# Attention keys with a meta key in front of every row, and right neighbours moved one element to the left by DMA

## The chip, the cores and the metric

The kernel runs on one NeuronCore of a Trainium2 chip. The metric is the device time of one execution in microseconds. The kernel is written with a framework that records instructions, finds their dependencies and writes the semaphores. The engines are TensorE (PE, with its weight loads PEld), VectorE (DVE), ScalarE (ACT), GpSimd (POOL) and SyncE (SP), which here only issues transfers. Each engine takes its instructions in a fixed order.

## The reference, cut to what matters

One layer of a bidirectional encoder: an input projection, then two branches side by side (a neighbourhood attention and a gated linear recurrence), a gated merge, an output projection and an MLP, over 1024 real tokens and 16 learned meta tokens. The change touches the attention alone. The tokens form a grid of 16 rows by 64 columns; a query attends to a clamped window of 8 rows by 16 columns around it, with a relative bias, and always to all 16 meta keys:

```python
col_start = jnp.clip(c - NA_WIN_W // 2, 0, GRID_W - NA_WIN_W)
in_win = (c[None, :] >= col_start[:, None]) & (c[None, :] < col_start[:, None] + NA_WIN_W)
s_win = jnp.where(in_win[:, None, :], s_win + bias[None], -1e30)
s_meta = jnp.einsum('brchd,bmhd->bhrcm', qg, km).astype(jnp.float32) * scale
s = jnp.concatenate([s_win.reshape(B, H, rows, GRID_W, kh * GRID_W), s_meta], axis=-1)
p = jax.nn.softmax(s, axis=-1).astype(v.dtype)
o_grid = (jnp.einsum('bhrcjw,brjwhd->brchd', p_win, v_blk)
          + jnp.einsum('bhrcm,bmhd->brchd', p_meta, vm)).reshape(B, T, H, dh)
```

There are 8 heads of 64. A query in column c sees columns c−8 to c+7, shifted inwards at the grid's edges.

## The kernel before, in words

All matrix products are in a rounded fp32 format with each operand split into a high and a low part; the product of the two low parts is left out.

**Stages.** The recurrence comes first (until about 340 us), then the attention with the projections of its queries, keys and values (until about 571 us), then the gates, the merge, the output projection and the MLP. Four head pairs are done one after the other in the attention (the loop over `p`, L766). A pair's projections (`proj`, L133) put out queries, keys and values in that order; the next pair's projections are there to fill PE while the present pair's softmax runs.

**Strips.** The 64 columns are cut into 8 strips of 8 columns. A strip holds 16 rows × 8 columns = 128 tokens, one full tile of partitions. A query strip `s` needs the key strips `s−1`, `s` and `s+1`; the edge strips 0 and 7 have two. `KS` and `KL` (high and low keys) hold for each strip 128 real keys and then 16 meta keys (`SW` = 144 columns), so that three strips are one run of 432 columns, of which only the centre strip's meta columns are unmasked. `QX` holds the query's high part on one half of the partitions and its low part on the other.

**Scores** (L831): two products into one bank (L838, L839), 432 columns wide (288 at the edges). DVE adds mask and bias from `NB` and takes the minimum (L844), ACT takes the exponent (L846), DVE scales (L847, L848).

**Values** (L851): the probabilities `pr` are turned block by block by transposes on PE (L859), with one more transpose that is shifted by 16 columns and so ends with the meta columns (L861). ACT copies the high part to `PH` and DVE the low part to `PL` (L870, L871). After every four strips (a group: 2 halves of strips × 2 heads in a pair) the products with the values follow: first and last with the ninth block of `V`, which holds the meta values in its last 16 rows and zeros elsewhere (L875, L884), in between with each block of `V` that the four strips see (L882, L883). `V` has nine blocks of 128 tokens (2 heads × (64 high + 64 low) columns); it is one buffer, filled for each pair by transposes of `vT` (L821) and copies by ACT and DVE (L823, L824).

**Order.** In this stage the order on the engines is not written out by hand (a written order for PE, ACT and DVE ends with the first pair's keys, `in_order.close()`). A planner puts an instruction on its engine when its inputs and buffers are ready by the planner's own reckoning, earlier code first; the order is fixed when the kernel is built. Transfers for weights (L102, L951), bias (`bs`, L770) and mask (`NB`, L771) are on SP's queue. A value step runs when three score steps stand ahead of it (`pend`, L892 to L896); there are five tiles of probabilities, two banks for scores, and one `PT` a head for high and one for low parts.

Of the kernel before, what the change touches and what calls it, by code (L numbers as in the profile page):

```python
# [9 lines left out]
F32 = mybir.dt.float32  # L10
F32R = mybir.dt.float32r
# [25 lines left out]
SW = P + NM  # L37

# [10 lines left out]
def layer(ctx: ExitStack, tc: tile.TileContext, x, meta, w_in, w_na, w_hg, w_o, w_up, w_dn,  # L49
# [697 lines left out]
    with (tc.tile_pool(name="npr", bufs=1, side="right", reuse_waits="tile") as npr,  # L747
# [5 lines left out]
        V = npr.tile([P, 9, 2, P], F32R, name="Vn")  # L753
        pool.memset(KL[0][64:128].bitcast(F32), 0.0)
        pool.memset(KL[1][0:64].bitcast(F32), 0.0)
        pool.memset(vT[:, 8], 0.0)

        def strips(t, p0, t0, n, w=None):

            a = t[p0:p0 + 64, 0:8, t0 // 8:(t0 + n) // 8]  # L760
            return a.rearrange("p s (r c) -> p s r c", c=8)

# [3 lines left out]
        for p in range(NPAIR):  # L766
            NB = npl.tile([P, 2, 1024], F32, tag="NB", name="NB")
            for i in range(2):
                bs = npl.tile([P, TH], F32, tag="bs", name="bs", bufs=3)[:, :384]
                sp.dma_start(bs, bias[:, (2 * p + i) * 384:(2 * p + i + 1) * 384])  # L770
                sp.dma_start(NB[:, i, :1008], wmask)  # L771
                for o, j0, m in ((0, 0, 3), (432, 1, 2), (720, 0, 2)):
                    a = NB[:, i, o:o + m * SW].rearrange("p (j c) -> p j c", c=SW)[:, :, :P]
                    pool.tensor_tensor(a, a, bs[:, j0 * P:(j0 + m) * P].rearrange("p (j c) -> p j c", c=P),
                                       op=ALU.subtract)
# [14 lines left out]
            def ev_k(ps, t0, n):  # L790
                for i in range(2):
                    act.copy(strips(KS[i], 64 * i, t0, n), grid(ps, 64 * i))
                for i in range(2):
                    b = 64 * i
                    dve.tensor_tensor(strips(KL[i], b, t0, n), grid(ps, b),
                                      strips(KS[i], b, t0, n).bitcast(F32), op=ALU.subtract)
                    act.copy(strips(KS[i], 64 - b, t0, n), strips(KS[i], b, t0, n).bitcast(F32))

            def mev_k(ps):
                for i in range(2):  # L800
                    b = 64 * i
                    m = ps[b:b + 64].unsqueeze(1).broadcast_to([64, 8, NM])
                    hi = KS[i][b:b + 64, :, P:]
                    act.copy(hi, m)
                    act.copy(KS[i][64 - b:128 - b, :, P:], m)
                    dve.tensor_tensor(KL[i][b:b + 64, :, P:], m, hi.bitcast(F32), op=ALU.subtract)
# [10 lines left out]
            for b in (0, 4, 8):  # L817
                pt = bank("t", "vpt")
                m = min(4, 9 - b)
# [4 lines left out]
                dve.tensor_tensor(V[:, b:b + m, :, 64:], src, V[:, b:b + m, :, :64].bitcast(F32), op=ALU.subtract)  # L824

# [5 lines left out]
            def scores(s, i):  # L831
                js = [j for j in (s - 1, s, s + 1) if 0 <= j < 8]
                w = len(js) * SW
                o = 432 if s == 0 else 720 if s == 7 else 0
                sc = bank("s", "nsc").rearrange("p a b -> p (a b)")
                ksl = KS[i][:, js[0]:js[-1] + 1].rearrange("p s c -> p (s c)")
                kll = KL[i][:, js[0]:js[-1] + 1].rearrange("p s c -> p (s c)")
                pe.matmul(sc[:, :w], QX[i][:, s], ksl, start=True, stop=False)  # L838
                pe.matmul(sc[:, :w], QX[i][:, s], kll, start=False, stop=True)  # L839
                pr = npr.tile([P, 432], F32, tag="pr", name="pr", bufs=5)  # L840
# [8 lines left out]
                return js, pr  # L849

            def values(s, i, js, pr):  # L851
                g, e = divmod(s, 4)
                if e == 0:
                    po[i] = [npr.tile([P, 22, P], F32R, tag=f"PT{q}", name=f"PT{q}") for q in range(2)]
                PH, PL = po[i]
                m = len(js)
                pt = bank("t", "ppt")
                for k in range(m):
                    pe.transpose(pt[:, k], pr[:, k * SW:k * SW + P], ident)  # L859
                cen = js.index(s)  # L860
                pe.transpose(pt[:, m], pr[:, cen * SW + NM:cen * SW + NM + P], ident)  # L861

                b0 = 3 * (js[0] - 4 * g) + e + 3
                if s < 7:
                    runs = [(0, m + 1, b0)]
                else:
                    runs = [(0, m, b0), (m, 1, 4 * e + 9)]
                for k, n, b in runs:
                    hi = PH[:, b:b + 3 * n - 2:3]
                    act.copy(hi, pt[:, k:k + n])  # L870
                    dve.tensor_tensor(PL[:, b:b + 3 * n - 2:3], pt[:, k:k + n], hi.bitcast(F32), op=ALU.subtract)  # L871
# [3 lines left out]
                pe.matmul(ov, V[:, 8, i], PH[:, 9:22:4], start=True, stop=False)  # L875
                for a in range(-1, 5):
                    j = 4 * g + a
                    if 0 <= j < 8:
                        es = [q for q in range(4) if abs(a - q) <= 1]
                        e0, ne = es[0], len(es)  # L880
                        b = 3 * a + e0 + 3
                        pe.matmul(ov[:, e0:e0 + ne], V[:, j, i], PH[:, b:b + ne], start=False, stop=False)  # L882
# [997 lines left out]
```

## Time and profile before

| what | value |
|---|---|
| time, median of 3 runs | 1510.95 us (1508.72 to 1511.25) |
| the profiled execution | 1510.21 us |
| its span, first to last instruction | 1508.4 us |
| PE busy | 1493.8 us, 99% of the span |
| DVE, ACT, POOL busy | 69%, 44%, 24% |
| mean granted TensorE clock | 0.999 |
| attention stage (340 to 571 us): PE, DVE, ACT busy | 228.87, 175.62, 144.91 of 231 us |

Busy time is the time in which an engine has at least one instruction under way. Matrix products overlap in their pipeline: what one of them holds PE for is the time from its start to the next one's start, not its listed duration. "Idle before, releaser" names what ended a wait. For transfers the page gives the number, the size and the median time from issue to landing.

### The profile page before, as it was taken

The page shows a single profiled execution, that of the slowest core. Times are in us where ns is not written, and L with a number is a line of the kernel's source. Part 1 is how long each engine was busy: PE and PEld are TensorE (multiplying, and loading weights), DVE is VectorE, ACT ScalarE, POOL GpSimd, SP SyncE. Part 2 cuts the span into 40 slices and gives each one's busy share as a digit, 9 for nine tenths or more (in the row PEclk, how much of TensorE's full clock was granted, in tenths as well). Part 3 has the DMA queues.
Part 4 walks back from the last instruction along what each step waited for, and adds up shares of the span by engine and source line. Part 5 has one row for each costly group of instructions (what it writes and reads, how often), then busy time and mean ns, then how long its engine had stood idle before and what let it go on. Part 6 is the DMA issues. An engine that isn't in the chain of part 4 may idle for free.

```text
span 1508.4 us, 23495 instructions
## 1 busy us (share of the span) xinstructions
PE 1493.8 (99%) x9200; PEld 1251.0 (83%) x9200; DVE 1036.5 (69%) x1624; ACT 664.7 (44%) x1185; POOL 366.3 (24%) x347
## 2 busy tenths in 40 slices
PE   9999999999999999999999999999999999999998
PEld 8888888888888888888888887888888888888886
DVE  7876666656786786675485479777777445877876
ACT  7131313135665576343233345555555534334444
POOL 3313031324414400110000121344444200231242
PEclk9999999999999999999999999999999999999999
DMA  4211011114223228444656124444444577563224
GB/s 170 60 29 58 29 47 40 44 29 133 83 68 95 98 75 274 140 141 159 231 167 223 42 94 164 168 154 154 153 154 154 202 254 234 189 230 114 97 84 154
DMA packets 142592, 195.62 MB, mean 130 GB/s; under 512 B 8192, under 2 KB 90368, under 8 KB 142480
## 3 DMA queue, kind: packets, MB, share of 16 engines
q1 hardware_dynamic: 133216, 172.86, 34.8%
q10 hardware_dynamic: 7088, 13.91, 2.4%
q0 software_dynamic: 2176, 7.34, 1.3%
q8 instruction: 72, 1.18, 0.3%
q14 instruction: 40, 0.33, 0.1%
HBM read 139.56 MB, written 54.53 MB: 129 GB/s over the span
## 4 chain that ended last, share of the span: by engine, by line
PE 89%; DVE 5%; ACT 2%; issue 2%; DMA 2%; POOL 1%; ACTq 0%; POOLq 0%; DVEq 0%
PE mm L122 10%; PE mm L123 10%; PE mm L124 10%; PE mm L1554 5%; PE pa L1554 5%; PE pb L918 4%; PE pb L919 4%; PE pb L920 4%; PE pb L1554 4%; PE pc L1554 4%; PE pc L919 3%; PE pc L920 3%; PE pc L918 3%; PE pa L920 2%; PE pa L919 2%
## 5 line engine op out<-in xcount | busy, mean ns | idle before, releaser
L122 PE MATMUL mm<-aT,hi 128*128 128x512 f32 (+2 forms) x600 | 213.9, 356 | 0.0
L123 PE MATMUL mm<-aT,hi 128*128 128x512 f32 (+2 forms) x600 | 211.9, 353 | 0.0
L124 PE MATMUL mm<-aT,lo 128*128 128x512 f32 (+2 forms) x600 | 211.7, 353 | 0.0
L97 DVE TENSOR_TENSOR dl<-ur,dh 128x1024 fp32r<-128x1024 f32 x54 | 71.0, 1315 | 87.4 <-ACT dh L96 87.2
L96 ACT CAST dh<-ur 128x1024 fp32r<-128x1024 f32 x54 | 56.9, 1054 | 166.7 <-issue 91.1
L122 PEld LDWEIGHTS mm<-aT,hi 128*128 128x128 f32 x600 | 113.2, 189 | 12.6
L124 PEld LDWEIGHTS mm<-aT,lo 128*128 128x128 f32 x600 | 113.2, 189 | 12.3
L123 PEld LDWEIGHTS mm<-aT,hi 128*128 128x128 f32 x600 | 113.2, 189 | 12.0
L1342 ACT ACTIVATE uv<-uv 128x512 f32<-128x512 f32 x48 | 30.4, 633 | 79.4 <-DVE uv L1450 52.8
L112 ACT CAST hi<-raw 128x1024 fp32r<-128x1024 f32 x26 | 27.3, 1051 | 77.2 <-PE mm L123 71.3
L844 DVE CUSTOM_DVE_ANT_0 pr<-nsc,NB 128x432 f32<-128x432 f32 (+1 forms) x64 | 35.2, 558 | 30.0 <-issue 21.6
L1645 POOL TENSOR_TENSOR w<-w,tt 128x512 f32<-128x512 f32 x16 | 23.4, 1461 | 133.1 <-DVE tt L1644 112.3
L300 POOL TENSOR_TENSOR Y<-X,TN 128x512 f32<-128x512 f32 x20 | 34.2, 1711 | 83.4 <-DVE X L297 83.4
L124 PE MATMUL mm<-o,lo 128*128 128x512 f32 x128 | 50.0, 391 | 0.2
L122 PE MATMUL mm<-wh,mT 128*128 128x512 f32 x128 | 50.2, 392 | 0.0
L123 PE MATMUL mm<-wl,mT 128*128 128x512 f32 x128 | 50.1, 391 | 0.0
L124 PE MATMUL mm<-wh,mT 128*128 128x512 f32 x128 | 49.9, 390 | 0.0
L123 PE MATMUL mm<-o,hi 128*128 128x512 f32 x128 | 49.8, 389 | 0.0
L122 PE MATMUL mm<-o,hi 128*128 128x512 f32 x128 | 49.8, 389 | 0.0
L1554 PE MATMUL mm<-dl,dh 128*128 128x512 f32 x124 | 48.6, 392 | 0.3 <-DVE dl L97 0.2
L1554 PE MATMUL mm<-dh,dl 128*128 128x512 f32 x124 | 48.3, 389 | 0.0
L1554 PE MATMUL mm<-dh 128*128 128x512 f32 x124 | 48.1, 390 | 0.0
(460 smaller groups left out, 4420.1 us busy)
## 6 DMA issues: line engine op xcount, KB each, us to landing
raw<-in_w_in SPq DMA_DIRECT2D x56, 512.0 KB, 4.0
ur<-usp SPq DMA_DIRECT2D x54, 512.0 KB, 3.5
raw<-in_w_up SPq DMA_DIRECT2D x16, 1024.0 KB, 6.0
usp<-us SPq DMA_DIRECT2D x60, 256.0 KB, 2.4
sg<-gsp SPq DMA_DIRECT2D x16, 512.0 KB, 4.7
w<-in_w_dn SPq DMA_DIRECT2D x16, 512.0 KB, 4.6
usp<-uv SPq DMA_DIRECT2D x30, 256.0 KB, 2.4
gsp<-gv ACTq DMA_DIRECT2D x24, 256.0 KB, 2.1
```

The lines of the kernel that those rows point to most:

```text
L96: act.copy(hi, src)
L97: dve.tensor_tensor(lo, src, hi.bitcast(F32), op=ALU.subtract)
L122: pe.matmul(ps, lh, rh, start=first, stop=False)
L123: pe.matmul(ps, lh, rl, start=False, stop=False)
L124: pe.matmul(ps, ll, rh, start=False, stop=last)
L300: pool.tensor_tensor(fap(Y, h, mid3), fap(X, h, mid3), fap(TT, 0, [[4, g], [n + 3, 2], [0, h]]), op=ALU.mult)
L844: dve.tensor_tensor_reduce(out=pr[:, :w], in0=sc[:, :w], in1=NB[:, i, o:o + w], scale=1.0, scalar=3.0e38, op0=ALU.add, op1=ALU.min, accum_ ...
L918: pe.matmul(ps, lhs[0][:, c], rhs[0][:, k], start=first and k == 0, stop=False, skip_group_check=True)
L919: pe.matmul(ps, lhs[0][:, c], rhs[1][:, k], start=False, stop=False, skip_group_check=True)
L920: pe.matmul(ps, lhs[1][:, c], rhs[0][:, k], start=False, stop=k == 3, skip_group_check=True)
L1342: act.activation(dst, src, AF.Relu)
L1554: pe.matmul(ps, a[n == 2][:, q, j * P:(j + 1) * P], b[n == 1][:, q], start=first and n == 0, stop=last and n == 2, skip_group_check=True)
```

## The change

Three things change in the attention; the rest of the kernel stays.

- **Keys in rows of nine.** For each strip and each grid row, `KS` and `KL` hold one meta key and then the 8 real keys (16 rows, 16 meta keys). All 128 real keys of a strip are read as elements 1 to 8 of each row, the 16 meta keys as element 0. Elements 0 to 7 of strip `s+1` are the 16 meta keys and the first 7 columns of the right neighbour, 128 columns in all. The eighth column of the right neighbour lies outside every window of an inner strip.
- **Scores** of an inner strip are 384 columns: 256 from the strips `s−1` and `s`, 128 from `s+1` read one element further left. Those of an edge strip are 272: 256 and 16 meta columns. Each part is a pair of products of its own, so a strip has four products where it had two. Mask and bias are laid out to match (`host_arrays`), with the bias in four blocks for a head.
- **Values.** An inner strip needs three transposes instead of four. The third block's products need the right neighbour's values in the same shifted order: row `n` of `VR` is row `n−1` of `V`, and rows 0, 8, 16, ... are the meta values. `VR` (six blocks, for strips 2 to 7) is filled by transfers from `V` on SP's queue. The meta block of `V` is used only for the edge strips.

```diff
+        VR = npr.tile([P, 6, 2, P], F32R, name="VR")
...
+        def key_strips(t, p0, t0, n):
+            a = t[p0:p0 + 64].rearrange("p s (r c) -> p s r c", c=RW)
+            return a[:, :, t0 // 64:(t0 + n) // 64, 1:]
+        def meta_of(a):
+            return a.rearrange("p s (r c) -> p s r c", c=RW)[..., 0]
...
-            for b in (0, 4, 8):
+            def right_values(j0, j1):
+                sp.dma_start(VR[1:, j0 - 2:j1 - 2].bitcast(F32), V[:P - 1, j0:j1].bitcast(F32))
+            def right_meta(j0, j1):
+                sp.dma_start(VR[0::8, j0 - 2:j1 - 2].bitcast(F32),
+                             V[P - NM:, 8:].bitcast(F32).broadcast_to([NM, j1 - j0, 2, P]))
+            for b, m in ((8, 1), (0, 4), (4, 4)):
                 pt = bank("t", "vpt")
-                m = min(4, 9 - b)
...
+                if b == 0:
+                    right_values(2, 4)
+            right_values(4, 5)
+            right_meta(2, 5)
+            right_values(5, 8)
+            right_meta(5, 8)
...
-                pe.matmul(sc[:, :w], QX[i][:, s], ksl, start=True, stop=False)
-                pe.matmul(sc[:, :w], QX[i][:, s], kll, start=False, stop=True)
-                pr = npr.tile([P, 432], F32, tag="pr", name="pr", bufs=5)
+                w, o = (3 * P, 0) if 0 < s < 7 else (EW, 3 * P + (EW if s else 0))
+                runs = []
+                for K in (KS, KL):
+                    k = K[i].rearrange("p s (r c) -> p s r c", c=RW)
+                    j = max(s - 1, 0)
+                    runs.append([k[:, s + 1, :, :8] if 0 < s < 7 else k[:, s, :, 0], k[:, j:j + 2, :, 1:]])
+                for dst, ks, kl in zip((scf[:, 2 * P:w], scf[:, :2 * P]), *runs):
+                    pe.matmul(dst, QX[i][:, s], ks, start=True, stop=False)
+                    pe.matmul(dst, QX[i][:, s], kl, start=False, stop=True)
...
-                for k in range(m):
-                    pe.transpose(pt[:, k], pr[:, k * SW:k * SW + P], ident)
-                cen = js.index(s)
-                pe.transpose(pt[:, m], pr[:, cen * SW + NM:cen * SW + NM + P], ident)
+                for k, c in enumerate((0, P, w - P)):
+                    pe.transpose(pt[:, k], pr[:, c:c + P], ident)
...
-                pe.matmul(ov, V[:, 8, i], PH[:, 9:22:4], start=True, stop=False)
-                for a in range(-1, 5):
...
-                pe.matmul(ov, V[:, 8, i], PL[:, 9:22:4], start=False, stop=True)
+                for a in (0, -1, 1, 2, 3):
+                    if 4 * g + a >= 0:
+                        e0 = max(a, 0) if a != 1 or g else 0
+                        add(V[:, 4 * g + a], 3 * a + e0 + 3, e0, min(a + 2, 4) - e0, start=a == 0)
+                for a in range(1 if g else 2, 4 if g else 5):
+                    add(VR[:, 4 * g + a - 2], 4 * a + 2, a - 1, 1)
+                add(V[:, 8], *((18, 3) if g else (9, 0)), 1, stop=True)
```

`add` (new) is a high product on all 128 columns of the block's weights and a low product on the first 64.

More of the change, by code (lines that the diff above doesn't have):

```diff
@@ L37 @@
 SW = P + NM
+RW = 9
+EW = 2 * P + NM
+NMASK = 3 * P + 2 * EW
 def fap(t, off, dims):
@@ L893, in layer @@
             for st in steps:
-                pend.append((*st, *scores(*st)))
+                pend.append((*st, scores(*st)))
                 if len(pend) > 2:
```

105 lines of the change are left out of this document (52 added, 53 removed).

## The prediction

> **What bounds the kernel now.** I read the engine totals first, then the granted clock over the stretch that the change touches (the attention stage, 340 to 571 us of the span), then the waits, the order of time inside that stretch, and the transfers.
>
> ```profile
> PE 1493.8 (99%) x9200; PEld 1251.0 (83%) x9200; DVE 1036.5 (69%) x1624; ACT 664.7 (44%) x1185; POOL 366.3 (24%) x347
> ```
>
> The second view is busy time by stretch; its columns are busy us (count) of PE, PEld, DVE, ACT, POOL, then the clock and the DMA share.
>
> ```profile
> 340.00:571.00 231.00, 228.87 (x1382) 196.15 (x1381) 175.62 (x436) 144.91 (x342) 75.89 (x74) 1.00 0.31 98
> ```
>
> PE is the bound, in the stage as in the whole: 228.87 of 231 us. DVE has 24% of the stage free and ACT 37%, so shorter work on them gives nothing by itself. PE works in order, and nearly every microsecond of it is a microsecond of the kernel; a wait put into PE's stream costs its full length too, if the work behind it isn't already placed in front.
>
> How long one PE instruction holds the engine is read from starts in the order of time, because the listed durations overlap. From pair 0, around its first value group, and the start of its third:
>
> ```profile
> 369.19 0.49 PE L859 MATMUL ppt<-ident,pr 128*128 128x128 f32 x3
> 369.52 0.27 PE L861 MATMUL ppt<-ident,pr 128*128 128x128 f32 x1
> ...
> 370.33 0.36 PE L838 MATMUL nsc<-KS,QX 128*128 128x432 f32 x1
> 370.52 0.36 PE L839 MATMUL nsc<-KL,QX 128*128 128x432 f32 x1
> 370.72 0.49 PE L859 MATMUL ppt<-ident,pr 128*128 128x128 f32 x3
> ...
> 373.54 0.48 PE L875 MATMUL pov<-PT,Vn 128*128 128x512 f32 x1
> 373.85 0.28 PE L882 MATMUL pov<-PT,Vn 128*128 128x256 f32 x1
> 373.97 0.28 PE L883 MATMUL pov<-PT,Vn 128*64 128x256 f32 x1
> 374.09 0.33 PE L882 MATMUL pov<-PT,Vn 128*128 128x384 f32 x1
> 374.26 0.34 PE L883 MATMUL pov<-PT,Vn 128*64 128x384 f32 x1
> ...
> 375.01 0.22 PE L882 MATMUL pov<-PT,Vn 128*128 128x128 f32 x1
> 375.07 0.22 PE L883 MATMUL pov<-PT,Vn 128*64 128x128 f32 x1
> 375.13 0.45 PE L884 MATMUL pov<-PT,Vn 128*128 128x512 f32 x1
> 375.42 0.27 PE L861 MATMUL ppt<-ident,pr 128*128 128x128 f32 x1
> ...
> 388.87 0.49 PE L875 MATMUL pov<-PT,Vn 128*128 128x512 f32 x1
> ```
>
> Start to start: a transpose 0.11 us ((369.52 − 369.19)/3), 432 columns 0.195 (mean of 0.19 and 0.20), 256 columns 0.12, 128 columns 0.06, so about 0.45 ns a column.
>
> **What the change takes off PE.** *Transposes.* An inner strip (6 of 8 strips, 2 heads, 4 pairs: 48 steps) goes from four transposes to three; an edge strip keeps three. 48 × 0.11 = 5.3 us.
>
> *Values.* A group of four strips now has 2 products of 4 blocks with the meta values and 22 blocks with V: 30 blocks of 128 columns. After the change: 8 blocks of left and centre values (e.g. 2+3+2+1), 3 of right values (VR) and one with V's ninth block, each in a high and a low product: 24 blocks. 6 × 0.06 = 0.36 us, 16 groups: 5.8 us. There are 16 or 18 products where there were 12, but the shortest keeps the pace of its columns (375.01 to 375.07). The two wide products took 0.31 and 0.29 us for 512 columns (4 × 0.06 = 0.24), which could give 0.12 × 16 = 1.9 us more; I leave it in the range.
>
> *Scores.* Inner: 2 × 432 columns become 2 × 256 and 2 × 128: 0.39 us become 0.24 + 0.12 = 0.36. 48 × 0.03 = 1.4 us. Edge: 2 × 288 (0.26 us at 0.45 ns) become 2 × 256 and two of only 16 columns. No row shows 16 columns here; between 0.01 us (by columns) and 0.06 (the shortest product above) each, so from no change to 0.10 us more a step. I take the slow end, as each also loads its weights: 16 × 0.10 = −1.6 us. Scores together: about nothing.
>
> The keys are now read with nine elements to a row, so in runs of eight. No row has that pattern; the nearest two stand in the recurrence, where L415 reads its moving operand in strides (down to single elements) and L394 in one run. Columns after the count: shortest/median/longest, ns.
>
> ```profile
> L415 PE MATMUL sc<-QQ,X x1664: 192/196/270, 57.9 to 315.7; 128*32 128x32 f32 x171, 128*64 128x64 f32 x14
> L394 PE MATMUL sc<-q,kd x256: 196/196/217, 57.4 to 284.6; 128*32 128x32 f32 x128
> ```
>
> The medians are equal, so I take nothing for it (bound: a loss of 1 ns in 32 columns, on some 45,500 columns that is 1.4 us).
>
> Sum off PE: 5.3 + 5.8 = **11 us** (9 to 14).
>
> Elsewhere: exponent, sums and scaling on 384 instead of 432 elements, and copies of three blocks instead of four, on DVE and ACT; both lie behind PE. POOL subtracts as many bias elements as before; the bias load grows by a third and the mask load shrinks, both far ahead of their use. If PE weren't full, these would matter first on DVE (76% of the stage).
>
> **What it adds: five transfers a pair on SP, and a wait of PE for them.** VR's rows 1 to 127 are V's rows 0 to 126, moved in three parts (blocks 2–3: 2 KB a row; block 4: 1 KB; blocks 5–7: 3 KB). Then the 16 rows 0, 8, ... are overwritten with meta values, in two transfers, each of which must wait for the parts that it overwrites. The three VR products close to each group's end wait for this. When can it start, and when is it needed?
>
> ```profile
> 365.35 1.07 ACT L823 CAST Vn<-vpt 128x512 fp32r<-128x512 f32 x2
> 365.97 1.29 DVE L824 TENSOR_TENSOR Vn<-vpt,Vn 128x512 fp32r<-128x512 f32 x2
> ...
> 368.69 0.28 DVE L824 TENSOR_TENSOR Vn<-vpt,Vn 128x128 fp32r<-128x128 f32 x1
> ```
>
> V's first four blocks are ready at 365.97 + 1.29/2 = 366.6, the next four at 367.3; the ninth block now goes first, which adds some 0.3: **366.9** and 367.6. The first group starts at 373.54; with the eight V blocks ahead of VR (16 × 0.06 = 1.0), plus 0.3 and less three transposes, PE comes to VR at **374.4**. So 7.5 us are covered by other work; what goes beyond them PE stands still for, since the planner has fixed its order and PT (one buffer a head), five probability tiles and two score banks let little run ahead.
>
> Now the length. Fixed part and rate come from these rows (KB each, us to landing; packets, MB, share of 16 engines):
>
> ```profile
> DMA packets 142592, 195.62 MB, mean 130 GB/s; under 512 B 8192, under 2 KB 90368, under 8 KB 142480
> q1 hardware_dynamic: 133216, 172.86, 34.8%
> q10 hardware_dynamic: 7088, 13.91, 2.4%
> osp<-ot SPq DMA_DIRECT2D x8, 256.0 KB, 2.1
> xm<-in_meta ACTq DMA_DIRECT2D x1, 64.0 KB, 3.1
> g_col<-in_g_mix ACTq DMA_DIRECT2D x1, 4.0 KB, 4.9
> lt<-in_lbl ACTq DMA_DIRECT2D x1, 8.0 KB, 6.5
> gain_sb<-in_gain ACTq DMA_DIRECT2D x1, 2.0 KB, 7.3
> ```
>
> One of the 16 engines moves 13.91 MB/(0.024 × 16 × 1508.4 us) = 24.0 GB/s while busy on the lightly used queue, 172.86/(0.348 × 16 × 1508.4) = 20.6 on SP's. Rows 1 to 127 are 127 × 6 KB = 780 KB. The fixed part is 2.1 us less 262 KB/(16 × 24) = 1.4 us.
>
> How 127 rows are dealt to the engines no row shows. Evenly over 16, the three parts take 780/(16 × 24) = 2.0 us: VR's first half is complete at 367.6 + 2.0 + 1.4 + 2.1 for the meta transfer = 373, before 374.4, and nothing waits. All on one engine, they take 780/24 = **32.5 us** (37.9 at 20.6). For the second end speaks the count of small packets: the transfers in the 43 rows of that view add up to 488; the last three rows above have 128 packets each (32, 64 and 16 B a row), and 8192 − 384 = 7808 = 16 × 488. So every transfer closes with one small packet on each of 16 engines: all were dealt out in 16 shares, and all have 128 or 16 rows, which 16 divides. 127 is prime; equal shares exist only for one engine. I take that end, 4 to 1 against uneven shares.
>
> [...]
>
> *Order on SP.* By the code the first meta transfer comes before the third part. But the planner puts on SP what is ready first:
>
> ```profile
> 359.82 3.84 SPq L770 DMA_DIRECT2D bs<-in_bias  x2
> 363.75 1.37 SPq L102 DMA_DIRECT2D raw<-in_w_in  x2
> 390.11 0.81 SPq L771 DMA_DIRECT2D NB<-in_wmask  x2
> ```
>
> The code issues bs, NB, bs, NB (L770, L771, per head); SP did bs, bs, two weight loads, NB, NB. The third part is ready with the second, the meta transfer only when both have landed. So all three parts go into the engine's line first, and the meta rows' share on it stands behind them. Behind the waiting meta transfer stand SP's next ones, here NB, wanted only by the next pair's scores.
>
> VR's first half is complete at 366.9 + 32.5 + 1.4 + 0.5 for the meta rows = 401.3. PE stands still 401.3 − 374.4 = **26.9 us** a pair. The second half (403) is there before the strips' second half wants it (the group of 388.87, moved to 415.8). V has one buffer and the next V block comes only after this pair's values, so each of four pairs pays: 108 us. After a long stop PE is slow, as at the kernel's start:
>
> ```profile
> 1.65 5.38 PE L583 MATMUL warm<-ident 128*128 128x128 f32 x24 [1.65 <-POOL ident masks.py:199]
> 7.59 0.88 PE L583 MATMUL warm<-ident 128*128 128x128 f32 x6
> ```
>
> (5.38 − 0.27)/23 = 0.22 us a transpose against (0.88 − 0.27)/5 = 0.12: up to 2.4 us lost in the first 5. I take 2 a pair, 8 us (0 to 10).
>
> Sum on the profiled execution (1510.21 us, its span 1508.4 and 1.8 around it, 0.7 below the median of 1510.95): 1510.2 − 11 + 108 + 8 = 1615; with some of it hidden, where the planner reckons with later arrival and puts the next pair's projections ahead (up to 5 us a pair, 20), 1595. I say **1612**.
>
> **The rivals.** *Code order on SP.* The first meta transfer goes ahead of the third part: first half at 366.9 + 390/24 + 1.4 + 2.1 = 386.7, PE waits 12.3; the third part starts at 384.8, its meta rows land at 384.8 + 16.3 + 1.4 + 2.1 = 404.6, where PE comes at 388.9 + 12.3 + 0.2: 3.2 more. 4 × 15.5 = 62; with the clock 1510.2 − 11 + 62 + 8 = **1569**. Against it: bs and NB above.
>
> *Shares over 16 engines (the other side).* The transfers land at 373, PE never waits, and what PE was spared is kept: 1510.2 − 11 = **1499**. For it: that the engines could take eight rows each, seven on one. It decides from a rate of all parts above 780/(7.5 − 3.5) = 195 GB/s, eight engines at 24. That the change does less than it says (runs of eight, edge products) reaches to 1505.
>
> *Shares over 16, but late.* SP stands at a weight load that waits for its buffer as V becomes ready, and the parts leave 5 us late: two or three us a pair, eating the gain: **1510**.
>
> **How the numbers follow.** One engine, parts first: 0.60, 1590 to 1640 (the upper end is 20.6 GB/s: 5.4 us a pair more). One engine, code order: 0.21, 1555 to 1590. Shares over 16: 0.15. Late: 0.04, half faster or slower and half the same. A difference of 0.2% (3 us) is about what a measurement of this kernel can tell from none. So slower 0.82, faster 0.15, same 0.03. The range 1545 to 1650 takes in both one-engine cases with their bounds, the chance left out being the 0.19 of the other two.
>
> **What would show it.** Right: PE idle before products with VR, once a pair, some 27 us, released by a transfer; SP's transfers to VR 13 to 35 us to landing; PE at half pace for some microseconds after each stop; transposes 192 where there were 240 and value columns down a fifth. A landing of 2 to 3 us proves the one-engine step wrong, and with it the sign. PE idle of 12 us twice would be code order. If transposes or 256-column products don't keep the paces above, the 11 us are wrong.

## The result and the profile after

The changed kernel takes **1644.88 us** (median of 6 runs, 1643.24 to 1646.28) where the kernel before, beside it, takes 1509.88 us: a ratio of 1.0893 [1.0879, 1.0907]. It is 135 us slower. The forecast was 1612 us with a range of 1545 to 1650: side, place and mechanism are as forecast, but 33 us are missing from the sum.

From the page of the changed kernel: engine totals, granted clock in 40 slices, the chain that ended last, and the value products with VR.

```profile
PE 1507.3 (92%) x9360; PEld 1267.5 (77%) x9360; DVE 1026.9 (63%) x1616; ACT 660.6 (40%) x1177; POOL 363.4 (22%) x347
...
PEclk9999999996969798899999999999999999999999
...
PE 78%; DMA 10%; DVE 5%; ACT 3%; issue 2%; POOL 1%; ACTq 0%; SPq 0%; POOLq 0%; DVEq 0%
...
L900 PE MATMUL pov<-PT,VR 128*128 128x128 f32 x48 | 11.8, 313 | 109.9 <-DMA VR<-Vn 109.9
```

The span is 1642.7 us, 134.3 longer. PE was to do less and shows more busy time (1507.3 instead of 1493.8), in 160 products more. Five slices show a clock of 0.6 to 0.8, one for each of the first three pairs and two for the last, and DMA has 10% of the chain.

PE's longest wait (engine, tile and line, what ended it; us in all, times, longest), and then PE and SP in the order of time in pair 0, two answers of one view:

```profile
PE pov L900 <- DMA VR<-Vn: 109.9, 4, 27.5
```

```profile
373.67 0.22 PE L902 MATMUL pov<-PT,Vn 128*64 128x128 f32 x1
401.31 0.48 PE L900 MATMUL pov<-PT,VR 128*128 128x128 f32 x1 [27.42 <-DMA VR<-Vn]
401.58 0.31 PE L902 MATMUL pov<-PT,VR 128*64 128x128 f32 x1
401.69 0.41 PE L900 MATMUL pov<-PT,VR 128*128 128x128 f32 x1
401.90 0.31 PE L902 MATMUL pov<-PT,VR 128*64 128x128 f32 x1
...
367.29 13.57 SPq L834 DMA_DIRECT2D VR<-Vn  x3
386.14 15.56 SPq L837 DMA_DIRECT2D VR<-Vn  x2
418.15 0.83 SPq L784 DMA_DIRECT2D NB<-in_wmask  x2
```

PE stops once a pair, for 27.5 us, ahead of the first product with VR, and a transfer releases it. On SP all three parts come first, then both meta transfers, and NB waits behind them, as the forecast put it.

Busy time by stretch, in the columns of the prediction: first around the stop, then what comes after the last value product, which ends at 691.43 us.

```profile
374.00:377.40 3.40, 0.00 (x0) 0.00 (x0) 1.89 (x7) 1.31 (x4) 0.00 (x0) 1.00 0.08 28
377.60:401.20 23.60, 0.00 (x0) 0.00 (x0) 0.00 (x0) 0.00 (x0) 0.00 (x0) 0.50 0.07 27
401.40:404.70 3.30, 3.30 (x18) 3.30 (x19) 1.78 (x4) 0.96 (x2) 0.00 (x0) 0.50 0.08 15
405.00:408.00 3.00, 3.00 (x23) 2.57 (x22) 2.27 (x8) 2.11 (x6) 0.00 (x0) 1.00 0.02 5
...
691.43:1642.70 951.27, 940.27 (x4170) 775.43 (x4169) 638.05 (x772) 420.69 (x648) 199.26 (x157) 1.00 0.49 165
```

During the stop the DMA share is 0.07, close to one engine of 16 (0.0625). The value products end at 691.4 us where they ended at 570.0. What follows takes 951 us for 4170 products; before it was 938 us for 4133:

```profile
570.04:1508.40 938.36, 930.04 (x4133) 767.04 (x4131) 633.94 (x770) 415.58 (x641) 199.25 (x157) 1.00 0.48 164
```

So 37 products that used to fill gaps in the attention now come after it, and these 951 us hold a fifth stretch at half clock (0.50 from 708.7 to 712.0). It isn't only the stop that lengthened the kernel.

**Where the 134 us are.** In the order of time I add up, for each PE product, the time from its start to the next one's start, by kind of product. The sums over all PE instructions make up the span, so their differences to the kernel before show where it grew. A wait is counted with the product that it follows; "all else" is projections, the other stages and the 1.7 us ahead of the first product.

| kernel | span, us | scores | transposes of pr | value products | V's transposes | all else |
|---|---|---|---|---|---|---|
| before, in us | 1508.4 | 26.7 | 21.7 | 30.3 | 6.4 | 1423.3 |
| after, difference | +134.3 | +16.5 | −2.3 | +115.6 | +1.3 | +3.2 |

Of the +115.6, 109.9 are the four stops. What is left, 5.7, together with the other columns is 24.4 us, where the forecast had 11 us saved and 8 lost to the clock.

### The profile page after: what moved, and what is told of

It reads as the page before. It is cut to its first block, busy times and chain, and to the rows that moved or that the text cites. A ratio compares the mean times of both kernels' runs of the same rounds, so it can differ in the third digit from the quotient of the medians.

```text
span 1642.7 us, 23875 instructions
## 1 busy us (share of the span) xinstructions
PE 1507.3 (92%) x9360; PEld 1267.5 (77%) x9360; DVE 1026.9 (63%) x1616; ACT 660.6 (40%) x1177; POOL 363.4 (22%) x347
## 4 chain that ended last, share of the span: by engine, by line
PE 78%; DMA 10%; DVE 5%; ACT 3%; issue 2%; POOL 1%; ACTq 0%; SPq 0%; POOLq 0%; DVEq 0%
PE mm L125 10%; PE mm L126 9%; PE mm L127 9%; DMA VR<-Vn 8%; PE mm L1581 4%; PE pa L1581 4%; PE pb L945 4%; PE pb L946 4%; PE pb L947 4%; PE pb L1581 4%; PE pc L1581 4%; PE pc L947 2%; PE pc L945 2%; PE pc L946 2%; PE pa L945 2%
## 5 line engine op out<-in xcount | busy, mean ns | idle before, releaser
L900 PE MATMUL pov<-PT,VR 128*128 128x128 f32 x48 | 11.8, 313 | 109.9 <-DMA VR<-Vn 109.9
L900 PEld LDWEIGHTS pov<-PT,VR 128*128 128x128 f32 x48 | 10.1, 220 | 110.4 <-DMA VR<-Vn 55.2
L893 ACT CAST PT<-ppt 128x384 fp32r<-128x384 f32 x64 | 29.3, 477 | 135.4 <-PE ppt L890 107.5
L913 DVE COPY low<-pov 64x512 f32<-64x512 f32 x16 | 11.1, 693 | 110.2 <-PE pov L902 110.0
L875 DVE CUSTOM_DVE_ANT_0 pr<-nsc,NB 128x384 f32<-128x384 f32 (+1 forms) x64 | 32.8, 519 | 34.9 <-issue 25.6
L786 POOL TENSOR_TENSOR NB<-NB,bs 128x384 f32<-128x384 f32 x8 | 8.4, 1051 | 192.6 <-DMA NB<-in_wmask 192.6
```

The costliest lines, as they stand in the source:

```text
L875: dve.tensor_tensor_reduce(out=pr[:, :w], in0=sc[:, :w], in1=NB[:, i, o:o + w], scale=1.0, scalar=3.0e38, op0=ALU.add, op1=ALU.min, accum_ ...
```

## The experiments

Ratios are against the kernel before on the same chip. In the second batch, from whole scores on, the expectations number their theories afresh.

**1. Two cuts: is it the row count?** Each part of VR goes as rows 0 to 111 and rows 112 to 126.

```diff
-                sp.dma_start(VR[1:, j0 - 2:j1 - 2].bitcast(F32), V[:P - 1, j0:j1].bitcast(F32))
+                for r0, r1 in ((0, 112), (112, 127)):
+                    sp.dma_start(VR[r0 + 1:r1 + 1, j0 - 2:j1 - 2].bitcast(F32), V[r0:r1, j0:j1].bitcast(F32))
```

> The changed kernel, with each part of the right values moved as two transfers (rows 0 to 111 and 112 to 126 of V, 112 and 15 rows). Theory 1, one engine for 127 rows: 112 rows have 16 equal shares and 15 rows 15, so the parts land in 2 to 4 us, the 109.9 us of PE idle before the first VR product go (under 2 us a pair remain) and with them the slow 3.5 us after each stop (4 x 1.75): 1645 - 110 - 7 = about 1528 us. If what the change takes off PE (11 us) had come too, it would be 1499. Rival: it is the amount, the SBUF-to-SBUF path or the meta transfers' waits that are slow, not the row count: the idle time stays over 20 us a pair and the time over 1600.

Measured: 1528.59 us, 1.0123 [1.0109, 1.0137]. From the list of transfers of that kernel, KB each and us to landing, the largest:

```profile
VR<-Vn SPq DMA_DIRECT2D x4, 336.0 KB, 3.3
```

No wait of PE for VR is left. The same bytes, in six transfers where there were three, give 116 us back, and the time is the one that theory 1 gave. But it is still 18.5 us slower than the kernel before beside it (1510.08 us), with no stop for VR and a clock of 1.00 over the attention: these are not waits for the transfers.

**2. Four row counts in one kernel.** Pairs 0 to 3 cut their parts after 127, 122, 123 and 112 rows.

```diff
-                sp.dma_start(VR[1:, j0 - 2:j1 - 2].bitcast(F32), V[:P - 1, j0:j1].bitcast(F32))
+                cut = (127, 122, 123, 112)[p]
+                for r0, r1 in ((0, cut), (cut, 127)):
+                    if r1 > r0:
+                        sp.dma_start(VR[r0 + 1:r1 + 1, j0 - 2:j1 - 2].bitcast(F32), V[r0:r1, j0:j1].bitcast(F32))
```

> The changed kernel, with the first cut of the rows different in each head pair: 127 rows (pair 0), 122 + 5 (pair 1), 123 + 4 (pair 2), 112 + 15 (pair 3). Theory 1, the largest number of engines up to 16 that divides the row count: 1, 2, 3 and 16 engines, so 780 KB x (rows/127)/(engines x 24 GB/s) = 32.5, 15.6, 10.5 and 1.8 us, and PE idle before the pair's first VR product of 27.5, 10.6, 5.5 and 0 us; the sum 44 against 109.9, the time about 1528 + 44 + 6 = 1578. Uneven shares (8 rows to an engine): pairs 1 and 2 wait no longer than pair 3. Amount or path: all four wait 27.

Measured: 1574.9 us (one run). PE's first products with VR in pairs 0, 1 and 2, from the order of time; pair 3 has no such wait:

```profile
401.95 0.47 PE L903 MATMUL pov<-PT,VR 128*128 128x128 f32 x1 [27.98 <-DMA VR<-Vn]
...
473.85 0.48 PE L903 MATMUL pov<-PT,VR 128*128 128x128 f32 x1 [10.46 <-DMA VR<-Vn]
...
541.43 0.44 PE L903 MATMUL pov<-PT,VR 128*128 128x128 f32 x1 [6.19 <-DMA VR<-Vn]
```

127 is prime, 122 = 2 × 61, 123 = 3 × 41, 112 = 16 × 7. The stops fall as if 1, 2, 3 and 16 engines shared the rows, each of them within 0.7 us of the expected 27.5, 10.6, 5.5 and 0. Five rows fewer in the largest transfer take 17.5 us off the stop. Busy time inside the three stops, in the same columns as above:

```profile
378.50:401.50 23.00, 0.00 (x0) 0.00 (x0) 0.00 (x0) 0.00 (x0) 0.00 (x0) 0.50 0.08 28
464.00:473.60 9.60, 0.00 (x0) 0.00 (x0) 0.41 (x1) 0.00 (x0) 0.00 (x0) 0.67 0.15 55
536.00:541.20 5.20, 0.00 (x0) 0.00 (x0) 0.26 (x1) 0.00 (x0) 0.00 (x0) 0.77 0.23 77
```

The DMA share is 0.08, 0.15 and 0.23, a little over one, two and three engines of 16 (0.06, 0.13, 0.19). The count of small packets, which left the question open in the prediction, settles it now. In the changed kernel's page:

```profile
DMA packets 144641, 199.35 MB, mean 121 GB/s; under 512 B 8332, under 2 KB 90376, under 8 KB 144528
```

That is 140 more under 512 B than before (8192). With one small packet for each share, the eight meta transfers of 16 rows give 8 × 16 = 128, and the twelve parts of 127 rows give the other 12: one share each. The same sum for this run (first cuts in 1, 2, 3 and 16 shares, their rests of 5, 4 and 15 rows in 5, 4 and 15) is 3 × 46 + 128 = 266, and for two cuts 12 × 31 + 128 = 500; their pages have 8458 and 8692, which is exactly that much more than 8192.

**3. Nothing moved.** VR is neither filled nor read; its products read V.

```diff
-                    add(VR[:, 4 * g + a - 2], 4 * a + 2, a - 1, 1)
+                    add(V[:, 4 * g + a], 4 * a + 2, a - 1, 1)
```

> The changed kernel without VR's transfers: the products with the right neighbours' values take the unshifted block of V instead of VR, so the right neighbours' and the meta keys' values are left wrong for inner strips; all products, transposes and softmax steps stay in number and size. It shows what the rest of the change does by itself. Working of the forecast: 1510 - 11 = 1499 (1496 to 1502). Theory 2, products of 128 columns and fewer are held to the pace of a 128-column weight load (0.11 us, not 0.06 or 0.01): the score steps cost 0.07 (inner) and 0.2 us (edge) more instead of nothing, that is 3.4 + 3.2, values give 3.8 instead of 5.8, transposes 5.3: 1510 - 2.5 = about 1507; with more waits among the finer pieces up to 1525.

Measured: 1537.54 us, 1.0180 [1.0166, 1.0194]. A miss: without any transfer it is 9 us slower than with two cuts. Its leading wait (with two cuts 6.2 us, 9 times):

```profile
PE ppt L884 <- DVE PT L888: 9.5, 7, 2.0
```

The traces say why. By what they write and read and by their shapes, this run's instructions on PE, DVE, ACT and POOL stand in the very order of the changed kernel; it is two cuts whose order is another. So the same products in two orders are 9.6 us of span apart. PE's idle time (the span less its busy time) is 6.7 us longer here than in two cuts. Its busy time is 2.8 us longer, and in four stretches of 3.4 us, the first from 377.7 to 381.1, the granted clock is 0.50; two cuts has none in the attention.

The run also prices the transfers with the order kept: 1642.7 − 1536.4 = 106.3 us of span. What is left, 28.0 us over the kernel before, is not the transfers, and it depends on the order.

**4. The kernel before, its inner scores split** into 288 and 144 columns, nothing else.

```diff
-                pe.matmul(sc[:, :w], QX[i][:, s], ksl, start=True, stop=False)
-                pe.matmul(sc[:, :w], QX[i][:, s], kll, start=False, stop=True)
+                for c0, c1 in ((288, w), (0, 288)):
+                    if c1 > c0:
+                        pe.matmul(sc[:, c0:c1], QX[i][:, s], ksl[:, c0:c1], start=True, stop=False)
+                        pe.matmul(sc[:, c0:c1], QX[i][:, s], kll[:, c0:c1], start=False, stop=True)
```

> The kernel before, with one thing done: the 432 score columns of an inner strip as products of 288 and 144 columns, four instead of two (96 x 2 more over the kernel); nothing else. Theory 2, pace of the weight load: 2 x (0.13 + 0.11) = 0.48 us instead of 0.39 on 48 steps, +4.3 us: 1514. By columns alone, as the forecast took it: no change, 1510.

Measured: 1532.53 us, 1.0147 [1.0134, 1.0161]. Splitting alone (96 products more) costs more than the whole change does with two cuts; both expected values miss. Its order of time, and in the changed kernel an inner strip, an edge strip and the short value products:

```profile
387.72 0.30 PE L840 MATMUL nsc<-KS,QX 128*128 128x144 f32 x1
387.85 0.28 PE L841 MATMUL nsc<-KL,QX 128*128 128x144 f32 x1
387.96 0.34 PE L840 MATMUL nsc<-KS,QX 128*128 128x288 f32 x1
388.14 0.30 PE L841 MATMUL nsc<-KL,QX 128*128 128x288 f32 x1
388.27 0.39 PE L122 MATMUL mm<-aT,hi 128*128 128x512 f32 x1
```

```profile
409.23 0.38 PE L868 MATMUL nsc<-KS,QX 128*128 128x256 f32 x1
409.44 0.30 PE L869 MATMUL nsc<-KL,QX 128*128 128x256 f32 x1
409.58 0.23 PE L868 MATMUL nsc<-KS,QX 128*128 128x128 f32 x1
409.64 0.28 PE L869 MATMUL nsc<-KL,QX 128*128 128x128 f32 x1
409.75 0.34 PE L868 MATMUL nsc<-KS,QX 128*128 128x256 f32 x1
...
414.28 0.29 PE L868 MATMUL nsc<-KS,QX 128*128 128x256 f32 x1
...
414.67 0.38 PE L868 MATMUL nsc<-KS,QX 128*128 128x256 f32 x1
...
415.12 0.28 PE L900 MATMUL pov<-PT,VR 128*128 128x128 f32 x1
415.24 0.22 PE L902 MATMUL pov<-PT,VR 128*64 128x128 f32 x1
415.30 0.27 PE L900 MATMUL pov<-PT,VR 128*128 128x128 f32 x1
415.41 0.22 PE L902 MATMUL pov<-PT,VR 128*64 128x128 f32 x1
```

Split, the inner scores hold PE for 0.55 us (387.72 to 388.27), not the 0.39 before; in the changed kernel it is 0.52 (409.23 to 409.75) for 48 columns fewer, and an edge strip takes 0.39 (414.28 to 414.67) instead of 0.26. In a run of short products, one with 128 columns of weights holds PE for 0.11 to 0.12 us and one with 64 for 0.06, although both have 128 moving columns: the load of the weights sets the pace in these rows. The loads themselves (PEld) start at 415.07, 415.18, 415.24, 415.35 and 415.41, so the next one follows 0.11 us after one of 128 columns and 0.06 after one of 64.

But 48 × 0.16 is 7.7 us, and the loss is 22. Of the rest, PE's idle time is 10.6 us longer than in the kernel before (25.2 us, not 14.6), and two stretches of 3.4 us outside the attention are at clock 0.50 (8.3 to 11.7 and 598.8 to 602.2), with PE busy throughout: some 3 us more, as an estimate.

**5. Whole scores, two cuts.** Rows of nine, three transposes, VR and its transfers stay. The scores read whole key strips in one run, as before, and the scaling picks the 384 elements. It writes them to a tile of its own, so that there are now four tiles of scaled probabilities and three of unscaled ones, where there were five.

```diff
-                for dst, ks, kl in zip((scf[:, 2 * P:w], scf[:, :2 * P]), *runs):
-                    pe.matmul(dst, QX[i][:, s], ks, start=True, stop=False)
-                    pe.matmul(dst, QX[i][:, s], kl, start=False, stop=True)
+                pe.matmul(sc[:, :w], QX[i][:, s], ksl, start=True, stop=False)
+                pe.matmul(sc[:, :w], QX[i][:, s], kll, start=False, stop=True)
...
-                dve.tensor_scalar(pr[:, :w], pr[:, :w], rc, None, op0=ALU.mult)
+                pq = pw[:, :w].rearrange("p (j r c) -> p j r c", j=n, c=RW)
+                dve.tensor_scalar(pr[:, :2 * P].rearrange("p (j r c) -> p j r c", j=2, c=8), pq[:, :2, :, 1:], rc,
+                                  None, op0=ALU.mult)
+                dve.tensor_scalar(pr[:, 2 * P:].rearrange("p (r c) -> p r c", c=8), pq[:, n - 1, :, :8], rc,
+                                  None, op0=ALU.mult)
```

> The keys in rows of nine, the three transposes, VR and its transfers are kept (each part of VR in two cuts of 112 and 15 rows); what is undone is the splitting of the score products: they read whole key strips in one run (432 columns, at the edges 288) as in the kernel before, and the scaling on VectorE, now two instructions, picks the 384 elements that are kept. Theory 1 (what the change loses on TensorE are the short score products, paced by their weight loads of 0.11 us): 48 transposes of 0.11 us less, 5.3 us, and in the values 2 to 4 us less (0.175 us for a short pair of products instead of 0.12), so 1510 - 8 = 1502 us, 1499 to 1506, and no wait of TensorE for a transfer. Rival (the loss is the order that the planner finds and the waits between engines, whatever the width of the products): 1515 to 1530 us, near the 1528.6 of the kernel with two cuts and split products.

Measured: 1518.48 us, 1.0058 [1.0045, 1.0070]. Whole scores are worth 10 us, and the scores' time is back (26.4 us against 26.7), but the gain of 8 us didn't come; the time is in the rival's range. PE is busy for 4 us less than before (1489.8 against 1493.8) in a span 8.6 us longer. One of its stops, in pair 1:

```profile
435.18 0.69 DVE L912 COPY low<-pov 64x512 f32<-64x512 f32 x1
...
435.90 0.56 DVE L893 TENSOR_TENSOR PT<-ppt,PT 128x384 fp32r<-128x384 f32 x1
436.38 0.67 DVE L914 TENSOR_TENSOR OT<-pov,low 64x512 f32<-64x512 f32 x1
436.61 0.52 PE L889 MATMUL ppt<-ident,pr 128*128 128x128 f32 x3 [0.92 <-DVE PT L893]
```

PE's next transposes want a bank that DVE frees with L893, and DVE has put the copy L912 first. Fourteen times a projection product is followed by more than 0.65 us without a start, 13.8 us in all (less 0.2 us for each product itself, here and below); in the kernel before twice.

**6. Whole scores, VR turned by TensorE.** A second copy of the values, shifted by one element, is turned by six more transposes a pair; no transfer.

```diff
+                    a = vS[64 * i:64 * i + 64].rearrange("p s (r c) -> p s r c", c=8)
+                    act.copy(a[:, :, t0 // 64:(t0 + n) // 64, 1:], grid(ps, 64 * i)[:, 2:, :, :7])
...
-            for b, m in ((8, 1), (0, 4), (4, 4)):
+            for dst, wt in ((V[:, 8:], vT[:, 8:]), (V[:, :4], vT[:, :4]), (VR[:, :3], vS[:, :3]),
+                            (V[:, 4:8], vT[:, 4:8]), (VR[:, 3:], vS[:, 3:])):
```

> As the run with whole scores and two cuts, but VR is not moved: a second copy of the transposed values, shifted by one element, is written by ScalarE and turned by TensorE, six transposes a pair more, and nothing is transferred. Theory 1: 24 transposes of 0.11 us, 2.6 us more than the run with two cuts: 1505 us, 1502 to 1509. Rival (order and waits): 1515 to 1535 us. If it is not slower than the run with two cuts, the five transfers a pair cost as much as six transposes and two evictions.

Measured: 1525.02 us, 1.0100 [1.0085, 1.0116]: 6.5 us more than with the transfers, and in the rival's range. The additional transposes take 2.2 us of them (V's transposes 8.67 instead of 6.44), close to the expected 2.6; the stops after projections grow from 13.8 to 18.9 us. Moved in 16 and 15 shares, VR is cheaper by DMA here, though the order differs too.

**7. The kernel before, its inner scores in 216 and 216 columns.**

```diff
-                pe.matmul(sc[:, :w], QX[i][:, s], ksl, start=True, stop=False)
-                pe.matmul(sc[:, :w], QX[i][:, s], kll, start=False, stop=True)
+                for c0, c1 in ((0, 216), (216, w)) if w == 432 else ((0, w),):
+                    pe.matmul(sc[:, c0:c1], QX[i][:, s], ksl[:, c0:c1], start=True, stop=False)
+                    pe.matmul(sc[:, c0:c1], QX[i][:, s], kll[:, c0:c1], start=False, stop=True)
```

> The kernel before, with the inner scores (432 columns) made by two pairs of products of 216 columns each instead of one pair of 432; the same columns and the same banks, 96 products more, as in the run with 288 and 144 (1532.5 us). Theory 1 (a product of few columns takes as long as its weight load, 0.11 us): 216 columns at 0.45 ns are 0.10 us, so four products take 0.44 instead of 0.39 us, 48 x 0.05 = 2.4 us; with a little for the first load of a strip, which waits: 1512 to 1518 us. Rival (each product more costs the same, whatever its width, by its load or its place in the order): 1528 to 1536 us.

Measured: 1560.02 us, 1.0332 [1.0318, 1.0346]. Both are wrong, by far. The order of time shows the expected pace, and beside it waits:

```profile
385.98 0.28 PE L840 MATMUL nsc<-KL,QX 128*128 128x216 f32 x1
386.10 0.27 PE L839 MATMUL nsc<-KS,QX 128*128 128x216 f32 x1
386.20 0.27 PE L840 MATMUL nsc<-KL,QX 128*128 128x216 f32 x1
387.65 0.37 PE L839 MATMUL nsc<-KS,QX 128*128 128x216 f32 x1 [1.17 <-DVE mn L845]
```

```profile
PE ppt L860 <- DVE pr L849: 12.0, 19, 1.4
PE nsc L839 <- DVE mn L845: 6.4, 11, 1.2
```

216 columns start 0.10 to 0.12 us apart, so the products themselves cost the 2.4 us. Of the other 48 us, some 30 are waits (PE is idle for 45.0 us, before for 14.6): PE comes to a score bank before DVE has read it, and to the transposes before the scaling, with no projection put in between. And the clock fell. One of six such stretches:

```profile
390.20:396.90 6.70, 6.24 (x26) 5.45 (x26) 4.37 (x15) 2.52 (x7) 0.00 (x0) 0.50 0.00 0
```

They sum to some 24 us, with PE busy for 22 of them; if half of that is lost, they cost up to 11 us, an estimate.

**8 to 10. Is VectorE the cause?** Its share over the stage hides that it is almost full while the strips run. Busy time by stretch of the kernel before and of that with whole scores:

```profile
433.00:445.00 12.00, 12.00 (x71) 9.66 (x69) 11.53 (x34) 7.51 (x19) 0.00 (x0) 1.00 0.01 2
```

```profile
433.00:445.00 12.00, 10.07 (x67) 8.26 (x67) 11.41 (x38) 6.66 (x19) 0.00 (x0) 1.00 0.02 5
```

So I moved the copy of the lower value sums from DVE to ACT, in three kernels: whole scores, before, two cuts.

```diff
-                dve.tensor_copy(low, ov[64:])
+                act.copy(low, ov[64:])
```

> The kernel with whole scores and two cuts (1518.5 us), with one instruction per value group put on another engine: the copy of the lower half of the value sums out of PSUM (0.69 us, 16 times) goes from VectorE to ScalarE. Theory 3 (what TensorE saves in a strip turns into waits because VectorE, busy 11.2 to 11.7 of each 12 us while the strips run, sets their pace; its copy stands ahead of the subtraction that frees the transposes' bank): most of the 12.5 us that TensorE waits in front of transposes and value products there goes, 1506 to 1511 us, and VectorE is less than full in the strips' stretches. Rival (the waits come from the order that was planned, whatever the load of VectorE): 1515 to 1525 us, with the same stops.

> The kernel before, with only that copy put on ScalarE. Theory 3: TensorE was never kept waiting there (its waits in the stage sum to some 3 us), so hardly a gain: 1506 to 1511 us. Rival (any edit of the stage gives another order, and with it stops): 1515 us or more.

> The changed kernel with two cuts (1528.6 us), with only that copy put on ScalarE. Theory 3: of its 18.5 us some 12 are stops over 0.65 us in front of transposes and value products, and these go; what is left is the time of the score products (16 us more than before by their starts, of which stops are 5): 1517 to 1521 us. Rival (planned order): 1525 to 1532 us.

Measured: whole scores 1515.25 us, 1.0033 [1.0020, 1.0045], 3 us better, with the stops still there (12 of them, 13.2 us). Before: 1512.74 us, 1.0017 [1.0008, 1.0026], a little worse. Two cuts: 1524.81 us, 1.0092 [1.0078, 1.0106]; here the stops after projections did go (8.0 to 3.3 us), and the time fell by only 3.8. Theory 3 misses all three times; only in the last kernel did the stops go as it says. The rival is right for whole scores alone: the kernel before got another order too, but two stops as before, and not the 1515 us or more, and two cuts ended just under the rival's range.

**11 and 12. More off VectorE.** The scaling of the third block goes to ACT too, without and with that copy.

```diff
-                dve.tensor_scalar(pr[:, 2 * P:].rearrange("p (r c) -> p r c", c=8), pq[:, n - 1, :, :8], rc,
-                                  None, op0=ALU.mult)
+                act.mul(pr[:, 2 * P:].rearrange("p (r c) -> p r c", c=8), pq[:, n - 1, :, :8], rc)
```

> The kernel with whole scores and two cuts (1518.5 us), with the scaling of the third block of each strip (0.28 us, 64 times, 18 us in all) taken from VectorE to ScalarE; the copy of the lower value sums stays on VectorE. VectorE's work on a strip falls from some 2.0 us to 1.7 us, under the 1.9 us of the kernel before. Theory 3 (VectorE sets the pace while the strips run, and the stops of TensorE, some 13 us, are its doing): most of the stops go, 1503 to 1511 us. Rival (the stops belong to the planned order, whatever the load of VectorE): 1514 to 1525 us, again with a dozen stops.

> The same, with the copy of the lower value sums on ScalarE too (that copy alone took the kernel with whole scores from 1518.5 to 1515.3 us). Theory 3: 1501 to 1508 us, unless ScalarE, some 29 us fuller, becomes the one that PE waits for. Rival: 1512 to 1522 us.

Measured: 1519.75 us, 1.0061 [1.0049, 1.0073], and 1517.60 us, 1.0050 [1.0037, 1.0062], both in the rival's range. The longest wait of the first, and the same stretch of the second:

```profile
PE ppt L888 <- DVE PT L892: 10.2, 11, 1.3
```

```profile
433.00:445.00 12.00, 10.15 (x64) 7.73 (x63) 10.26 (x33) 11.62 (x31) 0.00 (x0) 1.00 0.01 2
```

From whole scores to both on ACT, DVE's busy time in this stretch goes from 11.41 to 10.26 us, and PE's from 10.07 to no more than 10.15; ACT, now at 11.62, may have taken DVE's place there. Taking load off VectorE doesn't bring the 8 us, so VectorE's load alone, theory 3, isn't the cause of the loss. The rival, that the stops belong to the order that was planned, fits whole scores with the copy or with the scaling on ACT (12 stops each) but not two cuts with the copy on ACT, where they went. No run with whole scores kept the order and changed the rest, and none kept five tiles of probabilities, so what makes PE stop with whole scores stays open between the order, the chain through DVE and ACT, and the four tiles. No version beats the kernel before.

**The table of starts, all runs with an interval** (differences to before in us, worked out as in the first section; waits are in them):

| kernel | span | scores | transposes of pr | values | V's transposes | all else |
|---|---|---|---|---|---|---|
| two cuts | +18.4 | +16.3 | −4.0 | +2.4 | +1.9 | +1.8 |
| two cuts, copy on ACT | +14.6 | +13.5 | −3.8 | +3.9 | +1.6 | −0.6 |
| nothing moved | +28.0 | +23.4 | −3.7 | +3.3 | +1.6 | +3.4 |
| before, 288 + 144 | +23.4 | +11.5 | +1.0 | 0.0 | +0.4 | +10.5 |
| before, 216 + 216 | +51.0 | +46.1 | +6.0 | +4.1 | +0.4 | −5.6 |
| before, copy on ACT | +1.0 | −0.9 | −0.5 | 0.0 | 0.0 | +2.4 |
| whole scores, two cuts | +8.6 | −0.4 | −1.1 | +0.4 | 0.0 | +9.7 |
| whole scores, turned | +15.0 | −0.6 | −3.7 | +1.1 | +2.2 | +15.9 |
| whole, copy on ACT | +4.9 | −0.6 | −4.9 | +0.9 | −0.1 | +9.7 |
| whole, scaling on ACT | +10.3 | +1.3 | −4.0 | +1.2 | −0.1 | +11.9 |
| whole, both on ACT | +7.3 | +0.5 | −4.6 | +2.1 | −0.1 | +9.4 |

In the rows with split scores the loss is in the scores' column, or next to it; in those with whole scores it is all in "all else", where the stops are.

## Why the prediction was right, and where it wasn't

- **127 rows on one engine**: right. Ahead of the result it was my estimate from the count of small packets, at 4 to 1; the four row counts (stops of 27.98, 10.46, 6.19 us and none) and the small packets (12 for the twelve parts of 127 rows) show it.
- **The parts ahead of the meta transfers on SP**: right (367.29 three, 386.14 two); the rival with the order of the code is out. The meta rows took 15.1 us to landing, with two cuts 2.2: they stood behind the third part, as forecast.
- **The stop**: PE was to reach VR at 374.4 and go on at 401.3. It reached it at 373.9 and went on at 401.31. Four stops: 109.9 us for 108.
- **Half clock**: right in size. The rows by stretch show 0.50 from 401.4 to 404.7 and 1.00 from 405.0; the first VR products start 0.21 and 0.11 us apart (401.69 to 401.90, 401.58 to 401.69) where at full clock it is 0.11 and 0.06. In the other pairs the clock came back 4.3 to 4.9 us after the first VR product (at 493.6, 582.3 and 671.1). PE is busy for 17 us of the four ends; half of that, 8.5, is an estimate of the loss, for 8.
- **11 us off PE**: this is the step that failed. Two cuts, without stops and with a full clock, shows what stood in its place. *Transposes*: 4.0 us saved of 5.3. *Values*: not 5.8 saved but 2.4 lost. "The shortest keeps the pace of its columns" holds in these rows only for a short product that follows longer ones; the changed groups end in eight short ones in a row, 0.175 us for a pair of them and not 0.12, which is 16 × 4 × 0.055 = 3.5 us. The other 4.7 are not explained by this: the value products of 256 columns hold PE for 0.20 us on average in two cuts, before for 0.12. *Scores*: not "about nothing" but 16.3 lost. The rows above give 48 × 0.13 + 16 × 0.13 = 8.3 by the loads of the weights; 4.9 are stops over 0.65 us, and the last 3 are not told apart. *V's transposes*, 1.9, were not in the sum. With 1.8 elsewhere that is 18.4 more where the forecast had 11 less, a miss of 29. Two cuts has another order, though. Nothing moved has the changed kernel's own, and there the same term is 28.0 more: a miss of 39, about 10 of which the next point gives back.
- **Hidden 3 us** (1615 made 1612): PE did nothing else during a stop (0.00 us busy from 377.6 to 401.2), so no projection was put ahead. But the stops cover waits that the same order has without them: against nothing moved the transfers cost 106.3 us, where stops and half clock by themselves are 109.9 + 8.5 and the forecast had 108 + 8.
- **The other side**: the rival with shares over 16 engines was priced at 1499. Two cuts makes just that case, at 1528.6: had the transfers gone out in 16 shares, the side would still have been slower. The chance of 0.15 for faster (0.16 with its part of the late case) stood on the term that failed. That the total came out within the range is in part luck: a term that was off by 29 to 39 us still fitted under an upper end that had been carried to 1640 and 1650 for a slower DMA engine.

The rows quoted held the warning: a transpose, too, is a product of 128 columns with 128 columns of weights, and it took 0.11 us, not 0.06. I took the lower figure from a place where the load had a lead: the one for the product of 375.01 started at 374.89, 0.12 us ahead, under a product of 256 columns, and among the short ones of the changed kernel the load for 415.30 started at 415.24, 0.06 ahead. And "PE is full, so what it is spared is gained" was read from shares of the stage: with whole scores PE was spared 4 us and the kernel lost 8.6, since PE then waited for DVE at other places, in a new order of the work and with one tile of probabilities fewer.

## What to carry to other kernels

Count the rows of a transfer before its bytes: a part of 112 rows and a rest of 15 landed in 2 to 4 us, where with 127 rows at once PE stood still for 27. Price a product at the longer of its columns and its weight load (here, in a run of short ones, 128 moving columns took 0.11 to 0.12 us with 128 columns of weights and 0.06 with 64; 432 took 0.195), and take the pace from rows in which such products follow each other; cutting the 432-column products in two cost 22 to 50 us here. Where a planner sets the order, a saving of a few microseconds on the full engine is less than what a new order can cost (the same products in two orders were 9.6 us apart), so such an edit is a guess until the waits are read again.

## What the runs showed of the hardware

- Transfers of 127, 122, 123 and 112 rows went as if 1, 2, 3 and 16 engines shared them: stops of 27.98, 10.46, 6.19 us and none, DMA shares of 0.08, 0.15 and 0.23 in the three stops, and one small packet more for each share.
- PE's clock fell to 0.50 some 3.7 us into the first stop (1.00 until 377.4, 0.50 from 377.6, the last product ended at 373.89), 4.5 to 5.1 us into the others, and stayed there for 3.5 to 4.9 us after work came back.
- The clock also fell without a long stop. With halves of 216 columns PE waited in the attention for no more than 1.6 us at once, but in the 3.4 us ahead of each of the six stretches at 0.50 it was busy for only 1.65 to 1.92 us.
- I had not expected that two halves of 216 columns would cost 50 us and 288 and 144 cost 22, for the same 96 products more. The paces of the products explain 2 and 8 of them, PE's longer idle time 30 and 11.
